# Two query tiles per visit in the dilated attention, fewer statistics stores, and memory gating tied behind row maxima

## The chip, the cores and the metric

The kernel runs on one core of one Trainium2 chip. The core has five engines with instruction streams of their own: TensorE (PE in the profile) for matrix products and transposes, VectorE (DVE), ScalarE (ACT), GpSimd (POOL) and SyncE (SP), which here only issues transfers. They wait for one another through semaphores. PE writes its results to PSUM, which has eight banks of 128 x 512 float32 values; tiles in SBUF are 128 partitions high. The metric is device time in microseconds (us) for one execution, the median over several. A profile is one execution of its own, with its own time.

## The reference, cut to what matters

One encoder block over 1024 tokens of width 1024: a dilated window attention (branch a), a grouped-query attention (b) and an attention into 256 memory slots (m), each gated and projected, merged by gates, and projected once more.

```python
h = rms_norm(x, g_pre)
a_qkv, bq, bk, bv, mq, ga, gb, gm, mg = split(h @ w_in)
# a: three groups (window, dilation) = (128,1), (512,4), (2048,16), 8 heads of 64 each
for gi, (window, dil) in enumerate(A_GROUPS):
    o_g, lse_g = dilated_window_attention(aq[gi], ak[gi], av[gi], window, dil)
    # sc = q k / 8 in the band; m = max sc; p = exp(sc - m); l = sum p; o = p v / l; lse = m + log l
wts = softmax(stack(lses), axis=0)                # over the three groups
oa  = einsum('gbsh,gbshd->bshd', wts, stack(outs))
ob  = softmax(qb kb / 8) vb                       # 8 query heads on 2 key heads, with a row maximum
om  = softmax(qm km / sqrt(128)) vm               # 256 memory slots
ya, yb, ym = (oa*silu(ga)) @ w_a, (ob*silu(gb)) @ w_b, (om*silu(gm)) @ w_m
merged = sigmoid(mg0)*ya + sigmoid(mg1)*yb + sigmoid(mg2)*ym
out = x + rms_norm(merged @ w_out, g_post)
```

## The kernel before

Dense products are made in three terms of high and low parts, so one dense product of a 128 x 512 output is 12 matmuls over four k-blocks. The work stands in stages along the span, and PE carries all of them: the projections of the start, then the grouped-query attention (`b_att`, 222 to 467 us from the start of the span), woven with gate products; the large projections of q, k and v of the dilated branch with the merge gates (467 to 1068 us); the dilated attention, woven with the branch projections `y` (1068 to 1291 us); the remaining `y` products, and the output projection to the end.

A stage with attention is woven from two sources: a generator that yields, between its steps, a cost in TensorE time, and a queue of dense units, whose matmuls fill that cost. In the dilated stage a dense unit (`add_y`) has 24 matmuls in two halves, each half in one bank (`psd`). After a half, `y_evac` is put on a list (`pend`), which is emptied one entry at a time along the stage; it is a multiplication by the gate in place in PSUM, and then an addition to the accumulator, on DVE.

**The dilated stage.** There are twelve items: four pairs of heads times three dilations, named (p_, g). An item has eight query tiles T of 128 rows. For two tiles and two heads, `scores(b)` writes two PSUM banks (`pss1`). `soft(T)` runs on DVE: for each head one custom instruction adds the mask, copies the scores to `pra` and takes the extreme of the row; ACT then takes the exponential with the row sum. `trans(T)` transposes the exponentials on PE into a bank (`pst`) and copies them on DVE to `app`. `pv(b)` multiplies four tiles with the values into one bank (`pst`), which ACT copies to `og`. PSUM holds four banks for scores (`s1=4`), two of `pst` and two of the dense products. `plan(it, pre, nxt)` sets the order: for each T of 0 to 7 a `soft`, then at even T the `scores` of the next two tiles, then `trans` of the tile three back (LAG), then `combining(T)` and `tokens(T)`; `pv` stands at T = 3 and T = 7, `stats` of the item before at T = 2. Each `soft` carries the whole dense filling of its T.

**Statistics and weighing.** `stats` transposes row extremes and sums, and stores them from `sr` to DRAM (`std`) in 4 transfers (g = 0, 2) or 8 (g = 1), from SP, or for g = 2 and for item (3, 1) from ACT. For the pairs 0 to 2 `combine` fetches them back as `cpt`, computes shares, stores them to `wgd`, loads them spread over the partitions (`wgt`, two buffers) and weighs and sums the three outputs on POOL (`weigh`, `gate`), one step where `STEP_T` names that T. For the last pair, `rows` is loaded from `std` in four transfers, two at T = 2 and two at T = 6 of the last item; `shares_3` transposes it and carries on from there while the last `y` products run. `wide`, `first_two` and what follows them apply the weights with banks of `pss1` and `pst`.

**The grouped-query attention.** Per step, PE transposes keys by queries into a bank `tr`, and DVE takes a row maximum from it (`TENSOR_REDUCE bn<-tr`); with the bank still unread the next such product waits. `memory_load(k)` loads the two halves of an output and of a gate of the memory branch, and `memory_gate(k)` multiplies them (tiles `tb` and `tx`) on DVE and stores them. At the step numbers n = 112, 116, 130 and 132 a load is issued, at 128, 129, 137 and 139 a gate of both halves.

The order of the instructions on an engine is fixed when the program is built. `issue_after(x)` holds an instruction behind x in that order.

## Time and profile before

| | |
|---|---|
| median of 3 runs | 1426.65 us (1425.48 to 1427.89) |
| the profiled execution's own time | 1428.24 us |
| its span | 1426.4 us |
| PE busy | 1389.7 us, 97% |
| DVE busy | 1022.1 us, 72% |
| ACT busy | 658.7 us, 46% |
| POOL busy | 573.1 us, 40% |
| transfers | 212.30 MB, mean 149 GB/s |

Busy time of PE counts matmuls whose clock is low as well as those at full clock. The views by time stretch give busy time of each engine with the granted clock; the views of waits say for which instruction an engine stood, with the line that it waited for; the timeline gives single instructions or runs of the same.

### The profile page before, as it was taken

Reading aid. Unit: us, or ns where it says so; the run is one execution under the profiler, and the core shown is the slowest. Engines: PE = TensorE matmul, PEld = TensorE weight load, DVE = VectorE, ACT = ScalarE, POOL = GpSimd, SP = SyncE. Lnnn points to the kernel's source line nnn. Section 1 sums busy time; section 2 is a strip of 40 time slices with the busy share of each in tenths; the row PEclk is TensorE's granted clock in tenths of the full one; section 3 lists DMA queues with packets and bytes.
Section 4 is the critical chain, followed back from the end, with each engine's and each line's share of the span. In section 5 each row is a group of like instructions: output and inputs, shape, how many; then the busy total and the mean of one; then the engine's idle time right before and its main releaser. Section 6 shows DMA issues by size and latency. Waiting matters only on the chain.

```text
span 1426.4 us, 21831 instructions
## 1 busy us (share of the span) xinstructions
PE 1389.7 (97%) x7775; PEld 1110.5 (78%) x7775; DVE 1022.1 (72%) x1828; ACT 658.7 (46%) x1384; POOL 573.1 (40%) x440
## 2 busy tenths in 40 slices
PE   7999999999999999999999999999999999989997
PEld 7799986656656889888888888888887777767886
DVE  7768677767784697676877766677786556657977
ACT  6544365665545444333333333333345665642332
POOL 0416703766656000254565544455541263360003
PEclk9999999999999999999999999999999999999999
DMA  6356532322251787333333233333365577655455
GB/s 234 98 177 213 187 115 74 112 82 79 96 184 49 239 263 235 118 118 119 111 109 96 95 114 104 111 104 119 109 215 191 187 214 206 204 163 179 149 204 177
DMA packets 122013, 212.30 MB, mean 149 GB/s; under 512 B 32592, under 2 KB 61104, under 8 KB 121904
## 3 DMA queue, kind: packets, MB, share of 16 engines
q1 hardware_dynamic: 112240, 196.92, 42.4%
q10 hardware_dynamic: 9664, 14.00, 2.7%
q8 instruction: 61, 1.00, 0.3%
q14 instruction: 48, 0.39, 0.1%
HBM read 144.48 MB, written 66.38 MB: 148 GB/s over the span
## 4 chain that ended last, share of the span: by engine, by line
PE 87%; DVE 5%; ACT 2%; POOL 2%; DMA 2%; issue 2%; ACTq 0%; SPq 0%; DVEq 0%; POOLq 0%
PE s L1322 34%; PE d L1883 5%; PE s L1232 4%; PE s L2107 4%; PE ov L815 4%; PE sc L2025 3%; PE s L1283 3%; PE d L143 3%; PE d L145 3%; PE d L147 3%; PE s L1582 2%; PE tr L1654 2%; PE s L799 2%; PE s L800 2%; PE tr L781 2%
## 5 line engine op out<-in xcount | busy, mean ns | idle before, releaser
L806 POOL TENSOR_TENSOR bl<-bl,bp 128x512 f32<-128x512 f32 x96 | 131.0, 1365 | 59.1 <-ACT bp L802 53.8
L1322 PE MATMUL s<-hh,vS 128*128 128x512 f32 x400 | 133.4, 395 | 0.0
L1322 PE MATMUL s<-vA,vS 128*128 128x512 f32 x450 | 106.6, 390 | 0.0
L106 DVE TENSOR_TENSOR vS<-vot,vS 128x512 fp32r<-128x512 f32 x75 | 86.1, 1149 | 19.9 <-ACT vS L105 19.9
L1322 PEld LDWEIGHTS s<-vA,vS 128*128 128x128 f32 x450 | 84.5, 188 | 18.3
L802 ACT ACTIVATE bp<-s 128x512 f32<-128x512 f32 x128 | 75.9, 596 | 48.7 <-PE s L800 47.6
L1595 ACT ACTIVATE pra<-pra,sts 128x192 f32<-128x192 f32 (+2 forms) x176 | 75.3, 429 | 47.9 <-DVE sts L1594 45.1
L782 DVE TENSOR_REDUCE bn<-tr 128x1 f32<-128x512 f32 x128 | 85.1, 683 | 12.0 <-PE tr L781 10.8
L143 PE MATMUL d<-hh,wh 128*128 128x512 f32 x224 | 90.4, 404 | 2.5 <-DVE fth L216 2.5
L147 PE MATMUL d<-hh,wl 128*128 128x512 f32 x224 | 90.1, 402 | 0.0
L145 PE MATMUL d<-hl,wh 128*128 128x512 f32 x224 | 89.6, 400 | 0.0
L1322 PEld LDWEIGHTS s<-hh,vS 128*128 128x128 f32 x400 | 75.3, 188 | 17.7
L1322 PE MATMUL s<-hl,vS 128*128 128x512 f32 x200 | 79.1, 395 | 0.0
L1322 PE MATMUL s<-hh,wh 128*128 128x512 f32 x200 | 78.4, 392 | 0.0
L1322 PE MATMUL s<-hh,wl 128*128 128x512 f32 x200 | 78.4, 392 | 0.0
L1322 PE MATMUL s<-hl,wh 128*128 128x512 f32 x200 | 77.8, 389 | 0.0
L1633 DVE COPY app<-tr 128x384 f32<-128x384 f32 (+1 forms) x64 | 38.8, 606 | 45.9 <-PE tr L1621 25.2
L1326 ACT ACTIVATE vv<-s 128x512 f32<-128x512 f32 x50 | 30.0, 599 | 85.7 <-PE s L1322 59.2
L1066 POOL TENSOR_TENSOR vot<-wr 128x512 f32<-128x512 f32 x13 | 22.2, 1707 | 111.3 <-DVE wl L106 111.3
L815 PE MATMUL ov<-bp,VS 128*64 128x512 f32 x256 | 58.5, 598 | 0.0
L781 PE MATMUL tr<-KS,QH 128*128 128x512 f32 x128 | 52.2, 407 | 4.7 <-DVE bn L782 3.8
L1356 POOL TENSOR_TENSOR wh<-wr,wh 128x512 fp32r<-128x512 f32 x17 | 21.9, 1289 | 85.6 <-ACT wh L1355 85.6
(627 smaller groups left out, 4078.9 us busy)
## 6 DMA issues: line engine op xcount, KB each, us to landing
wr<-in_wu SPq DMA_DIRECT2D x40, 512.0 KB
vA<-in_wu SPq DMA_DIRECT2D x24, 512.0 KB
qkd<-ko SPq DMA_DIRECT2D x96, 128.0 KB
wl<-thd SPq DMA_DIRECT2D x24, 512.0 KB
wos<-os SPq DMA_DIRECT2D x12, 512.0 KB
wr<-in_wbr SPq DMA_DIRECT2D x24, 256.0 KB
aq<-qkd SPq DMA_DIRECT2D x12, 512.0 KB
ak<-qkd SPq DMA_DIRECT2D x12, 512.0 KB
```

The source lines that it names most:

```text
L106: V.tensor_tensor(dst_l, src, dst_h.bitcast(F32), op=OP.subtract)
L143: PE.matmul(dst, wh[:, k, :], hh[k][:, t], start=k == 0, stop=False)
L145: PE.matmul(dst, wh[:, k, :], hl[k][:, t], start=False, stop=False)
L147: PE.matmul(dst, wl[:, k, :], hh[k][:, t], start=False, stop=k == 7)
L781: PE.matmul(s, QH[:, kv * 4 + j], KS[:, kv, c * 512:c * 512 + 512], start=True, stop=True)
L782: fp["last"] = V.tensor_reduce(st[i]["n"][:, j, c:c + 1], s, axis=AX.X, op=OP.min)
L802: A.activation(pp, s, AF.Exp, scale=-1.0)
L806: G.tensor_tensor(lsum[i % 2], lsum[i % 2], pp, op=OP.add)
L815: PE.matmul(o[e * 64:e * 64 + 64], VS[:, kt, kv], d.pop(kt), start=kt < 2, stop=kt >= NT - 2)
L1322: PE.matmul(BANK[n, c], a, b, start=k == 0 and q == 0 and not more, stop=k == 3 and q == 2, skip_group_check=c in "XW")
L1595: A.activation(src, src, AF.Exp, scale=-1.0, bias=bias, accum_out=sts[:, h, 1, T:T + 1])
L1883: PE.matmul(ps_, a, b, start=k == 0 and q == 0, stop=k == 3 and q == 2)
```

## The change

In the dilated stage `plan` no longer has eight visits of one tile, but four `visit(b)` of two tiles. One visit holds, in this order on PE, `pv` of the item before (at b = 0 and 2), `scores(b)`, and the transposes of two tiles of two visits back; on DVE the four `soft` heads, and then the two copies, which `trans` now returns as a function. `stats` stands at b = 1. Behind a visit two `rest(T)` hold `combining` and `tokens`. A visit has the filling cost of one T of before, each `rest` half of it, so that an item's sum is the same. PSUM is divided anew: two banks for scores instead of four, four of `pst` instead of two. `wide(g, x)` with x = 1 takes a `pst` bank.

Statistics are stored in 4, 4 and 1 transfers for g = 0, 1 and 2, all from SP, to `std` in another order of its dimensions; `rows` is loaded in two transfers of 32 partitions. `weigh` of g = 1 and 2 is split in a multiplication and an addition, each a step of its own, and `STEP_T` has 14 entries. The evacuation of a `y` half with an accumulation is two entries of the list `pend` instead of one. In `b_att`, each half of a memory gate is a call of its own, at n = 115 to 134, and is held behind the row maximum that was last issued.

```diff
-            std = dram.tile([4, 2, 3, 2, S], F32, name="std")
+            std = dram.tile([4, 3, 2, 2, S], F32, name="std")
...
-        def memory_gate(k):
-            for j, (o, g) in enumerate(zip(*MT.pop(k))):
+        def memory_gate(k, j):
+            o, g = [x[j] for x in MT[k]]
+            with tc.issue_after(fp["last"].ins):
                 V.scalar_tensor_tensor(o, o, 0.5, g, op0=OP.mult, op1=OP.mult)
-                nc.sync.dma_start(od[2, k, :, half[j]], o)
+            nc.sync.dma_start(od[2, k, :, half[j]], o)
+        MEMORY = {108: (0,), 110: (1,), 115: (0, 0), 117: (0, 1), 119: (1, 0), 121: (1, 1), 122: (2,), 124: (3,),
+                  129: (2, 0), 130: (2, 1), 133: (3, 0), 134: (3, 1)}
...
-    phase_psum("ps_a", s1=4, t=2)
-    pss1()
+    phase_psum("ps_a", s1=2, t=4)
...
-                V.tensor_copy(pp[:, :k], tp[:, :k])
                 st[T] = terms
+                return lambda: V.tensor_copy(pp[:, :k], tp[:, :k])
...
-                E = nc.scalar if g == 2 or (p_, g) == (3, 1) else nc.sync
+                dst = std[p_, g].rearrange("s h x -> (s h) x")
+                if g == 0:
+                    for z in range(4):
+                        nc.sync.dma_start(dst[z].rearrange("(b t a) -> t b a", b=16, t=8),
+                                          sr[8 * z:8 * z + 8].rearrange("p (b a) -> p b a", b=16))
+                elif g == 1:
+                    for z in range(4):
+                        nc.sync.dma_start(dst[z].rearrange("(e t a) -> t e a", e=4, t=8),
+                                          sr[8 * z:8 * z + 8].rearrange("p (e a) -> p e a", e=4))
+                else:
+                    nc.sync.dma_start(dst.rearrange("z (t a) -> (z t) a", t=8), sr)
...
+            def visit(b):
+                if pre and b in (0, 2):
+                    pre["pv"](b // 2)
+                if it:
+                    it["scores"](b)
+                at = it if b > 1 else pre
+                copies = [at["trans"](2 * ((b + 2) % 4) + j) for j in range(2)] if at and (it or b < 2) else []
+                if it:
+                    it["soft"](2 * b)
+                    it["soft"](2 * b + 1)
+                for f in copies:
+                    f()
+                if b == 1 and pre and it:
+                    pre["stats"]()
+                if not it:
+                    shares_3(b)
+                    return
+                if b in (0, 2):
+                    it["values"](b // 2)
+                if b == 2 and pre:
+                    ready()
+                if b == 3 and it["ahead"]:
+                    qk_fetch(*it["ahead"])
+            def rest(T):
+                combining(T)
+                tokens(T)
+            for b in range(4):
+                out.append((lambda b=b: visit(b), SOFT + 100.0 if it else LAST_PAD))
+                if it:
+                    out += [(lambda T=T: rest(T), 0.5 * SOFT + 50.0) for T in (2 * b, 2 * b + 1)]
...
-        STEP_T = (4, 0, 1, 1, 2, 6, 6, 7, 2, 3, 4, 6)
+        STEP_T = (4, 0, 1, 1, 2, 5, 6, 7, 7, 0, 3, 4, 5, 7)
...
-                    pend.append(lambda t=t, ps_=ps_: y_evac(m, t, ps_))
+                    pend.extend([lambda t=t, ps_=ps_, z=z: y_evac(m, t, ps_, (z,)) for z in range(1 if n == 0 else 2)])
...
-            W3B[g, x] = pst().rearrange("p a b -> p (a b)") if g == 2 else pss1()
+            W3B[g, x] = pst().rearrange("p a b -> p (a b)") if g == 2 or x else pss1()
```

The order of instructions shows three places. The first is PE in an item with g = 0 or 1, around a `pv`; `s` is a score product, `tr<-cs,pra` a transpose, `tr<-app,avs` and `avp` the outputs, `d` the dense products. Before:

```order
L1621 MATMUL tr<-cs,pra 128x128 x3
L1883 MATMUL d<-hh_86,wh 128x512
L1883 MATMUL d<-hh_87,wh 128x512
L1883 MATMUL d<-hl_95,wh 128x512
L1621 MATMUL tr<-cs,pra 128x128 x3
L1654 MATMUL tr<-app,avs 64x128 x14
L1654 MATMUL tr<-app,avp 64x128 x2
L1883 MATMUL d<-hh_87,wh 128x512
L1883 MATMUL d<-hh_88,wh 128x512
L1883 MATMUL d<-hl_96,wh 128x512
L1582 MATMUL s_10739<-ak,aq 128x128
L1582 MATMUL s_10740<-ak,aq 128x192
```

And the same item after:

```order
L1880 MATMUL d<-hh_88,wh 128x512
L1880 MATMUL d<-hl_96,wh 128x512
L1659 MATMUL tr<-app,avs 64x128 x14
L1659 MATMUL tr<-app,avp 64x128 x2
L1587 MATMUL s_10707<-ak,aq 128x128
L1587 MATMUL s_10708<-ak,aq 128x192
L1587 MATMUL s_10707<-ak,aq 128x64
L1587 MATMUL s_10707<-ak,aq 128x192
L1587 MATMUL s_10708<-ak,aq 128x128
L1587 MATMUL s_10708<-ak,aq 128x64
L1626 MATMUL tr<-cs,pra 128x128 x6
L1880 MATMUL d<-hh_88,wh 128x512
```

Outputs, scores and the transposes of two tiles now follow one another, with the dense products before and behind them. The second place is DVE in `b_att` near the first memory gates (`tx`, `tb`); `bn<-tr` are the row maxima, `QL` a part of the query preparation. Before:

```order
L106 TENSOR_TENSOR bll<-bl_2695,blh 128x512
L767 SCALAR_TENSOR_TENSOR tb_4576<-tb_4576,tb_4578 128x512
L717 TENSOR_TENSOR QL<-tr,QH 64x4x128 x2
L767 SCALAR_TENSOR_TENSOR tx_4520<-tx_4520,tx_4521 128x512 x2
L818 TENSOR_TENSOR obt<-obt,ov 64x512
L767 SCALAR_TENSOR_TENSOR tb_4577<-tb_4577,tb_4579 128x512
L782 TENSOR_REDUCE bn_4380<-tr 128x1 x2
```

After:

```order
L786 TENSOR_REDUCE bn_4529<-tr 128x1
L768 SCALAR_TENSOR_TENSOR tx_4446<-tx_4446,tx_4447 128x512
L786 TENSOR_REDUCE bn_4529<-tr 128x1 x2
L768 SCALAR_TENSOR_TENSOR tx_4446<-tx_4446,tx_4447 128x512
L106 TENSOR_TENSOR bll<-bl_2694,blh 128x512
L216 SCALAR_TENSOR_TENSOR fth<-d,fth 128x512
L822 TENSOR_TENSOR obt<-obt,ov 64x512
L786 TENSOR_REDUCE bn_4529<-tr 128x1 x2
L768 SCALAR_TENSOR_TENSOR tb_4492<-tb_4492,tb_4494 128x512
```

The gates stand singly with row maxima between them. The third place is SP near the end of the last item; `rows<-std` is the load that `shares_3` needs, `wgt<-g2d` loads a gate, `wl<-thd` and `wr` serve the `y` products. Before:

```order
L1524 DMA avs<-vdr 64x8x64 x2
L1825 DMA wgt<-g2d 128x1024
L1726 DMA rows<-std 16x128 x2
L1524 DMA avs<-vdr 64x8x64 x2
L1350 DMA wr<-in_wbr 128x512
L1363 DMA wl<-thd 128x1024
L1723 DMA wgt<-g2d 128x1024
L1726 DMA rows<-std 16x128 x2
```

After:

```order
L1529 DMA avs<-vdr 64x8x64 x2
L1822 DMA wgt<-g2d 128x1024
L1687 DMA std<-sr 8x4x32 x4
L1723 DMA rows<-std 32x128
L1352 DMA wr<-in_wbr 128x512
L1529 DMA avs<-vdr 64x8x64 x2
L1365 DMA wl<-thd 128x1024
L1720 DMA wgt<-g2d 128x1024
L1723 DMA rows<-std 32x128
```

The four stores now stand on SP ahead of the first load of `rows`, and the second load keeps its place behind the same large transfers.

More of the change, by code (lines that the diff above doesn't have):

```diff
@@ L858, in b_att @@
                     yield 109
-                if n in (112, 116, 130, 132):
-                    memory_load((112, 116, 130, 132).index(n))
-                if n in (128, 129, 137, 139):
-                    memory_gate((128, 129, 137, 139).index(n))
+                if n in MEMORY:
+                    (memory_gate if len(MEMORY[n]) > 1 else memory_load)(*MEMORY[n])
                 m = n - LAG_T
@@ L1363, in th_load, with y_evac @@
             nc.sync.dma_start(THS[m], thd[8 * i + f])
-    def y_evac(m, t, ps_):
+    def y_evac(m, t, ps_, parts=(0, 1)):
         n, i, f = steps[m]
@@ L1368, in y_evac @@
         if n == 0:
+            if 0 not in parts:
+                return
             if accs[f] is None:
@@ L1372, in y_evac @@
         else:
-            V.scalar_tensor_tensor(ps_, th[:, t], 1.0, ps_, op0=OP.add, op1=OP.mult)
-            V.tensor_tensor(accs[f][:, t], ps_, accs[f][:, t], op=OP.add)
+            if 0 in parts:
+                V.scalar_tensor_tensor(ps_, th[:, t], 1.0, ps_, op0=OP.add, op1=OP.mult)
+            if 1 in parts:
+                V.tensor_tensor(accs[f][:, t], ps_, accs[f][:, t], op=OP.add)
     def qk_first(x):
@@ L1591, in soft @@
                     src = pr[:, h * n:h * n + n]
-                    bias = sts[:, h, 0, T:T + 1]
+                    bias = sts[:, 0, h, T:T + 1]
                     m0 = 384 + 192 * h if turned(T, h) else mo
                     fp["last"] = V.tensor_tensor_reduce(src, sv[h], mask[:, m0:m0 + n], 1.0, 3.0e38, OP.add, OP.min, bias)
-                    A.activation(src, src, AF.Exp, scale=-1.0, bias=bias, accum_out=sts[:, h, 1, T:T + 1])
+                    A.activation(src, src, AF.Exp, scale=-1.0, bias=bias, accum_out=sts[:, 1, h, T:T + 1])
                 st[T] = pr
@@ L1607, in trans @@
                             st[T - 1 + z] = pp[:, z]
-                        V.tensor_copy(pp[:, :2], tp[:, :2])
-                    return
+                        return lambda: V.tensor_copy(pp[:, :2], tp[:, :2])
+                    return lambda: None
                 pr = st[T]
@@ L1674, in stats @@
                     A.activation(sr, tp[0:32, 0, :], AF.Copy)
-                E = nc.scalar if g == 2 or (p_, g) == (3, 1) else nc.sync
-                for h in range(2):
-                    for q in range(2):
-                        row = sr[(h * 2 + q) * 8:(h * 2 + q) * 8 + 8]
-                        dst = std[p_, h, g, q]
-                        if g == 0:
-                            E.dma_start(dst.rearrange("(b t a) -> t b a", b=16, t=8),
-                                              row.rearrange("p (b a) -> p b a", b=16))
-                        elif g == 1:
-                            for f in range(2):
-                                E.dma_start(dst.rearrange("(e r f a) -> f r e a", e=4, r=4, f=2)[f],
-                                                  row[f:f + 7:2].rearrange("p (e a) -> p e a", e=4))
-                        else:
-                            E.dma_start(dst.rearrange("(t a) -> t a", t=8), row)
+                dst = std[p_, g].rearrange("s h x -> (s h) x")
[9 more added lines that the diff above has]
+                    nc.sync.dma_start(dst.rearrange("z (t a) -> (z t) a", t=8), sr)
             return dict(
@@ L1692, in item @@
                 ahead=seq[p_ * 3 + g + 2] if p_ * 3 + g + 2 < len(seq) else None,
-                values=[(lambda x=x: values(x), 0.0) for x in range(2)],
-                scores=[(lambda b=b: scores(b), 0.0) for b in range(4)],
-                soft=[(lambda T=T: soft(T), SOFT + 100.0) for T in range(NT)],
-                trans=[(lambda T=T: trans(T), 0.0) for T in range(NT)],
-                pv=[(lambda b=b: pv(b), 0.0) for b in range(2)],
-                stats=(stats, 0.0))
+                values=values, scores=scores, soft=soft, trans=trans, pv=pv, stats=stats)
         def plan(it, pre, nxt):
@@ L1724, in tokens @@
                     if T in (2, 6):
-                        for j in (0, 1) if T == 2 else (2, 3):
-                            nc.sync.dma_start(rows[16 * j:16 * j + 16],
-                                              std[3, j % 2, j // 2].rearrange("s (t a) -> (s t) a", t=NT))
+                        j = T // 6
+                        nc.sync.dma_start(rows[32 * j:32 * j + 32], std[3, j].rearrange("s h (t a) -> (s h t) a", t=NT))
             def ready():
@@ L1731, in ready @@
                     todo.extend(combine(pre["key"][0], [OG.pop((pre["key"][0], x)) for x in range(3)]))
-            if it and not pre:
-                out += it["scores"][:2]
-            for T in range(NT if it else 4):
+            def visit(b):
+                if pre and b in (0, 2):
+                    pre["pv"](b // 2)
                 if it:
-                    out.append(it["soft"][T])
-                if T == 2 and pre and it:
-                    out.append(pre["stats"])
-                if T % 2 == 0 and (it or T == 0):
-                    x = {0: pre and it and it["scores"][1], 2: it and it["scores"][2], 4: it and it["scores"][3],
-                         6: nxt and nxt["scores"][0]}[T]
-                    if x:
-                        out.append(x)
-                if T < LAG:
-                    if pre:
-                        out.append(pre["trans"][T + 8 - LAG])
-                elif it:
-                    out.append(it["trans"][T - LAG])
-                out.append((lambda T=T: combining(T), 0.0))
-                out.append((lambda T=T: tokens(T), 0.0) if it else (lambda T=T: shares_3(T), LAST_PAD))
-                if T == 3:
-                    if pre:
-                        out.append(pre["pv"][1])
-                    if it:
-                        out.append(it["values"][1])
-                    if pre and it:
-                        out.append((ready, 0.0))
-                if T == 5 and it and it["ahead"]:
-                    out.append((lambda: qk_fetch(*it["ahead"]), 0.0))
-                if T == 7:
-                    out.append(it["pv"][0])
-                    if nxt:
-                        out.append(nxt["values"][0])
@@ new lines, in visit @@
+                    it["scores"](b)
[10 more added lines that the diff above has]
+                    shares_3(b)
+                    return
@@ L1787, in fetch @@
                 for h in range(2):
-                    E.dma_start(c["t"][h * 64:h * 64 + 64], std[p_, h].rearrange("g s (i e) -> i g s e", e=16))
+                    E.dma_start(c["t"][h * 64:h * 64 + 64].rearrange("p g s e -> p (g s) e"), std[p_, :, :, h].rearrange("g s (i e) -> i (g s) e", e=16))
             def shares():
@@ L1811, in put, with weigh @@
                     E.dma_start(wgd[p_, h].rearrange("g (i e) -> i g e", e=16), c["e"][h * 64:h * 64 + 64])
-            def weigh(g):
+            def weigh(g, add=False):
                 wv = wgt[g].rearrange("p (b a) -> p a b", b=16)
                 ogv, og0 = [z.rearrange("p (a b) -> p a b", b=16) for z in (ogs[g], ogs[0])]
-                G.tensor_tensor(ogv, ogv, wv, op=OP.mult)
-                if g:
+                if add:
                     G.tensor_tensor(og0, og0, ogv, op=OP.add)
+                else:
+                    G.tensor_tensor(ogv, ogv, wv, op=OP.mult)
             def gate():
@@ L1833, in combine @@
             return [fetch, shares, weights, put, lambda: [load(0), load(1)], lambda: weigh(0), lambda: weigh(1),
-                    lambda: load(2), load_gate, lambda: weigh(2), gate, store]
+                    lambda: weigh(1, True), lambda: load(2), load_gate, lambda: weigh(2), lambda: weigh(2, True), gate, store]
         todo = []
-        STEP_T = (4, 0, 1, 1, 2, 6, 6, 7, 2, 3, 4, 6)
+        STEP_T = (4, 0, 1, 1, 2, 5, 6, 7, 7, 0, 3, 4, 5, 7)
         seq = [(p_, g) for p_ in range(4) for g in range(3)]
@@ L1891, in first @@
         def first():
-            items[0]["values"][0][0]()
             yield FIRST_PAD
@@ L1923, in shares_3 @@
                 V.tensor_copy(c3[:, 0:2].rearrange("p g h s t -> p (g h s t)"), C["b"][:, 0:64])
-                V.tensor_tensor(mn, b[:, 0:4].rearrange("p (g h) (s t) -> p g h s t", g=2, s=2)[:, 0, :, 0], c3[:, 1, :, 0], op=OP.min)
-                V.tensor_tensor(mn, mn, c3[:, 2, :, 0], op=OP.min)
-                V.tensor_tensor(eg, c3[:, :, :, 0], mn[:, None].to_broadcast([P, 3, 2, NT]), op=OP.subtract)
+                V.tensor_tensor(mn, b[:, 0].rearrange("p (h t) -> p h t", h=2), c3[:, 1, 0], op=OP.min)
+                V.tensor_tensor(mn, mn, c3[:, 2, 0], op=OP.min)
+                V.tensor_tensor(eg, c3[:, :, 0], mn[:, None].to_broadcast([P, 3, 2, NT]), op=OP.subtract)
                 A.activation(eg, eg, AF.Exp, scale=-1.0)
@@ L1930, in shares_3 @@
                 b = C["b"][:, 0:192].rearrange("p (x y) -> p x y", x=12)
-                V.tensor_tensor(b[:, 8:11].rearrange("p g (h t) -> p g h t", h=2), eg, c3[:, :, :, 1], op=OP.mult)
+                V.tensor_tensor(b[:, 8:11].rearrange("p g (h t) -> p g h t", h=2), eg, c3[:, :, 1], op=OP.mult)
                 ds_ = cb.tile([P, 16], F32, name="cds", bufs=2)
```

## The prediction

> **What bounds the kernel now.** I read the page first, then the table of time stretches, then what PE waits for in the stages that the change touches, and last the timelines around those waits. The page gives the busy shares:

> ```profile
> span 1426.4 us, 21831 instructions
> PE 1389.7 (97%) x7775; PEld 1110.5 (78%) x7775; DVE 1022.1 (72%) x1828; ACT 658.7 (46%) x1384; POOL 573.1 (40%) x440
> ```

> PE is the bound. A change that removes no matmul can therefore win only where PE stands, where it steps slowly, or where its clock is low. The stretches (columns: length, busy time of PE, PEld, DVE, ACT, POOL with instruction counts, granted clock, DMA share, GB/s) show where that is:

> ```profile
> 222.00:467.00 245.00, 240.16 (x1031) 153.40 (x1030) 173.53 (x264) 140.58 (x233) 151.58 (x112) 0.99 0.28 95
> 467.00:1068.00 601.00, 601.00 (x2778) 499.00 (x2777) 446.08 (x521) 231.22 (x368) 248.65 (x149) 1.00 0.44 141
> 1068.00:1297.00 229.00, 215.85 (x2023) 164.53 (x2021) 141.97 (x569) 128.20 (x461) 85.44 (x42) 0.98 0.63 193
> 412.10:418.90 6.80, 5.13 (x13) 3.91 (x14) 4.81 (x9) 1.69 (x3) 2.26 (x3) 0.50 0.49 130
> 1272.30:1279.10 6.80, 4.29 (x12) 3.32 (x13) 3.40 (x12) 0.94 (x4) 0.00 (x0) 0.50 0.30 104
> 1296.20:1303.00 6.80, 5.74 (x14) 4.51 (x15) 6.63 (x12) 3.75 (x7) 0.00 (x0) 0.50 0.95 356
> ```

> From 467 to 1068 us PE has no gap, and the change touches nothing there. The grouped-query stage (first row) has 4.8 us without PE work, the dilated stage (third row) 13.2 us. The last three rows are stretches with the clock at half. What PE waits for, in three windows (400 to 467, 1268 to 1305, and 1072 to 1268 us; total, times, longest):

> ```profile
> PE tr L781 <- DVE bn L782: 3.3, 1, 3.3
> ...
> PE s L1922 <- DMA rows<-std: 5.1, 1, 5.1
> PE sc L2025 <- DVE og L1968: 3.1, 1, 3.1
> ...
> PE tr L1621 <- DVE app L1633: 2.2, 3, 1.3
> PE s L1582 <- DVE sts L1594: 1.0, 1, 1.0
> PE tr L1647 <- DVE app L1633: 0.7, 1, 0.7
> PE tr L1606 <- ACT pra L1595: 0.6, 2, 0.3
> PE s L1575 <- DVE sts L1594: 0.5, 1, 0.5
> ```

> Three single waits of 3.3, 5.1 and 3.1 us, and small ones of 5.0 us in all. Each of the three is followed by one of the half-clock stretches. What half clock costs shows in the chain of waits: six dense matmuls behind the second wait took 2.86 us, six shortly after it 1.40.

> ```profile
> 1268.23 6.29 DMA rows<-std
> ...
> 1274.81 0.34 PE s L1922
> 1275.15 2.86 PE d L1883 x6
> ...
> 1280.29 1.40 PE d L1883 x6
> ```

> So a half-clock stretch loses half of the PE busy time in it: 2.6, 2.1 and 2.9 us by the rows above. The three places together cost 3.3 + 2.6 = 5.9, 5.1 + 2.1 = 7.2, and 3.1 + 2.9 = 6.0 us.

> [...]

> **The change, part by part.** *Memory gates.* The first wait is DVE's doing. Its timeline there:

> ```profile
> 407.80 1.39 DVE L717 TENSOR_TENSOR QL<-tr,QH 64x512 fp32r<-64x512 f32 x2 [2.13 <-ACT QH L714]
> 409.22 2.23 DVE L767 SCALAR_TENSOR_TENSOR tx<-tx,tx 128x512 f32<-128x512 f32 x2
> 411.48 0.68 DVE L818 TENSOR_TENSOR obt<-obt,ov 64x512 f32<-64x512 f32 x1
> 412.08 1.03 DVE L767 SCALAR_TENSOR_TENSOR tb<-tb,tb 128x512 f32<-128x512 f32 x1
> 413.04 1.28 DVE L782 TENSOR_REDUCE bn<-tr 128x1 f32<-128x512 f32 x2
> ```

> Three gate halves, 2.23 + 1.03 us, stand between the maxima that PE waits for: just the 3.3 us that it stood. In the new order each half follows one row maximum, so a later maximum is delayed by one half (0.7 to 1.1 us), not by three. Gain: at most 5.9 us; at least none, if a gate halts DVE on its load, which is issued only some seven steps earlier. Near the end three halves still stand ahead of one `QL`. I take 5.5.

> *Fewer changes of kind on PE.* In the order, dense matmuls are resumed behind other work 88 times before and 48 times after, from the first scores to the transpose of `rows`. The price of one, from a stretch of PE's timeline:

> ```profile
> 1195.44 0.39 PE L1654 MATMUL tr<-app,avp 128*64 128x128 f32 x4
> 1195.76 0.50 PE L1883 MATMUL d<-bl,wh 128*128 128x512 f32 x1
> 1196.10 0.63 PE L1883 MATMUL d<-bh,wh 128*128 128x512 f32 x2
> 1196.56 0.40 PE L1883 MATMUL d<-bl,wh 128*128 128x512 f32 x1
> 1196.89 1.04 PE L1582 MATMUL s<-ak,aq 64*128 64x128 f32 x12
> 1197.86 0.55 PE L1621 MATMUL tr<-cs,pra 128*128 128x128 f32 x3
> 1198.16 0.71 PE L1883 MATMUL d<-bh,wh 128*128 128x512 f32 x2
> 1198.71 0.39 PE L1883 MATMUL d<-bl,wh 128*128 128x512 f32 x1
> 1198.94 0.49 PE L1621 MATMUL tr<-cs,pra 128*128 128x128 f32 x3
> ```

> A dense matmul steps by 0.23 us (1198.71 to 1198.94, 1196.10 to 1196.56 for two). The first behind outputs takes 0.34 (1195.76 to 1196.10), two behind transposes 0.55 instead of 0.46, the last ahead of scores 0.33. An interruption thus costs about 0.1 us at one of its ends: 40 x 0.1 = 4.0 us. Outputs directly ahead of scores, 22 times, have no row; by the nearest, 0.33 against 0.23, they cost the same 0.1, which is in those that remain on either side. Ends: 0, and 6 if both ends of an interruption count where outputs are moved.

> *Scores with one pair of banks.* `scores(b+1)` now waits for both `soft` of the same pair of banks, in the visit just before, no longer for those of two visits before. The rows for DVE:

> ```profile
> L1594 DVE CUSTOM_DVE_ANT_0 pra<-s,mask x192: 211/349/422, 1073.8 to 1266.3; 128x192 f32<-128x192 f32 x80, 128x64 f32<-128x64 f32 x64, 128x256 f32<-128x256 f32 x48
> L1633 DVE COPY app<-tr x64: 550/558/692, 1079.4 to 1259.0; 128x384 f32<-128x384 f32 x40, 128x512 f32<-128x512 f32 x24
> ```

> DVE needs 4 x 0.35 = 1.4 us for the softs of a visit. PE meanwhile has two tiles' transposes (six or eight, some 0.6 us by 0.30 per three) and six to eight dense matmuls (8 x 0.23 = 1.8): 2.0 to 2.4 us, and 1.8 more where `pv` comes first. So 0.6 to 1.0 us is left at half of the visits. A copy (0.56) or one evacuation ahead of the softs fits; both do not. I put 2.5 us for new waits here; ends 0, and 36 visits x 0.5 = 18.

> *Small waits.* The five rows above (5.0 us) stand where copies or softs are late. Copies now come a visit ahead of `pv`, behind which four `pst` banks instead of two wait: I take 2 us of the 5 as gone (ends 0 and 5).

> *Stores, loads of `rows`, and weighing.* Eight stores of item (3, 1) held up ACT, and SP waited for them before its next loads:

> ```profile
> 1259.08 5.32 ACTq L1685 DMA_DIRECT2D std<-sr  x8
> 1264.44 0.35 ACT L1595 ACTIVATE pra<-pra,c 128x64 f32<-128x64 f32 x1 [5.39 <-DVE c L1594]
> ...
> SPq L1524 <- DMA std<-sr: 2.4, 1, 2.4
> ...
> L1685 SPq DMA_DIRECT2D std<-sr x24: 589/590/754, 1110.1 to 1215.2; - x24
> ```

> Now ACT issues none, and four stand on SP: 4 x 0.59 = 2.4 us there, as much as the wait of SP that goes, but at an earlier step. What is won is ACT's 5.3 us: exponentials stood behind the stores, the outputs behind those, and the load of the next values, two places ahead of `rows` on SP, behind the outputs. I expect the second `rows` load about 4 us earlier (between 0 and 5.3). The two halves of a `weigh` leave the order of the transfers ahead of it as it is. PE has about 0.6 us less work between that load's place and the transpose of `rows`, since two tiles' transposes and the outputs are through earlier. So 5.1 - 4 + 0.6 = 1.7 us remain; behind a wait of 1.3 us, the longest of the small ones, no half-clock stretch stands, and I count none here. Gain 7.2 - 1.7 = 5.5 us, which I take. Ends: 0, if the load goes out as late as before, and 7.2.

> *The evacuation in two entries.* The same two instructions, but the bank is released later, some three steps of dense work before its next use. It costs nothing as long as DVE is not behind; if it is, the price is up to one 0.7 us operation for each of eight units, 5.6 us. I take 0.5.

> *The third wait.* The product at L2025 waits for a combine chain on DVE whose instructions are the same. DVE is busy for 6.63 of the 6.80 us in the third half-clock row. Nothing here makes it shorter: 0.

> **Sum:** 5.5 + 4.0 + 2.0 + 5.5 - 2.5 - 0.5 = 14.0 us. The profiled execution took 1428.2 us, so 1414.2 by its own time. It stood 1.6 us above the median of 1426.65, which gives 1412.6 for the median.

> **Rivals.** (A) *Slower: single score banks.* DVE's queue falls behind in most visits, and each `scores` waits. For it: 0.6 us of slack at half the visits, and 142 us of DVE work in 229. Against it: single waits of PE for softs were two in the whole stage, 1.5 us. It decides against the change from about 0.4 us per visit over 36 visits beyond what I took (14.0 us); at 0.55 us (19.8) the time is 1432.4.

> (B) *The `rows` wait stays.* SP now issues the stores itself, the second load stays behind wr, wl and wgt, and the 6.29 us from issue to landing is mostly the queue of large transfers. PE, arriving earlier, stands as long: 5.5 us of the sum go, 1418.1. A middle case, with 2 to 3 us left and the low clock with it, ends near 1415.

> (C) *The gates halt DVE on their loads.* The wait moves from three gates in a row to single ones: 5.5 us go, 1418.1.

> (D) *Changes of kind are not worth their price* and the new waits eat the rest: only gates and `rows` pay (11.0 us), 1415.6.

> (E) *The planning does not take effect*: B, C and D at once, 1426 to 1428.

> **How the numbers follow.** My forecast, 1405 to 1415.5: 0.50. B 0.14, C 0.09, D 0.10, all faster. A 0.13, of which 0.10 lies above 1429.5 and 0.03 within the band; E 0.04, half within the band and half faster. A measurement of this kernel tells 0.2% (2.9 us) from no change. So faster 0.85, same 0.05, slower 0.10. The range takes in B, C and D and a part of A: 1402 (all gains at their upper ends but the third wait: 5.9 + 6 + 5 + 7.2 = 24.1) to 1424.

> **What would show it.** Right: in the grouped-query stage PE is without the 3.3 us wait and the 0.50 clock near 412 us; the dilated stage shrinks from 229 us by 9 to 10; the wait for `rows` is at most 1.5 us, and the clock stays full behind it; the wait at L2025's successor is still about 3 us. Wrong: rows that say PE `s` waits for DVE `sts` many times (A); the `rows` wait at 3 to 5 us (B); DVE waits for transfers at the gates (C); a dilated stage with few waits, but no shorter (D).

## The result and the profile after

The changed kernel takes 1413.94 us in the median of four runs (1412.71 to 1415.53), the kernel before 1426.78 us. The ratio is 0.9911, with a 95% interval of 0.9894 to 0.9928: 12.8 us faster. The forecast was 1412.6, in a range of 1402 to 1424. The profiled execution is one of 1412.7 us, against 1428.2 before. The page of the changed kernel begins:

```profile
span 1410.9 us, 21845 instructions
...
PE 1379.7 (98%) x7775; PEld 1106.2 (78%) x7775; DVE 1025.7 (73%) x1828; ACT 658.5 (47%) x1384; POOL 574.7 (41%) x440
```

PE still bounds the kernel. What it waits for between 150 and 1340 us (total, times, longest):

```profile
PE sc L2021 <- DVE og L1964: 2.7, 1, 2.7
PE d L1880 <- DMA wgt<-wgd: 2.2, 1, 2.2
PE tr L1659 <- DVE app L1639: 1.7, 1, 1.7
PE s L1918 <- issue: 1.0, 1, 1.0
PE d L1880 <- DVE acc L1380: 0.9, 1, 0.9
PE s L804 <- DVE QL L794: 0.9, 1, 0.9
...
PE tr L785 <- DVE bn L786: 0.7, 2, 0.5
PE tr L793 <- DVE bnm L788: 0.4, 1, 0.4
```

The waits of 3.3 us for row maxima and 5.1 us for `rows` are gone (what is left of the latter is the 1.0 us at L1918), and the third, now 2.7, is there. But three new ones stand in the dilated stage (2.2, 1.7, 0.9) and one in the grouped-query stage (0.9). Four lines mark the stages; each row has the first and the last start of a group. Before, the first large projection, the first `y` product, the transpose of `rows` and the first product of the tail:

```profile
L1232 PE MATMUL s<-wh,hh x56: 389/389/393, 467.6 to 538.5; 128*128 128x512 f32 x56
L1883 PE MATMUL d<-hh,wh x128: 387/396/504, 1067.7 to 1176.1; 128*128 128x512 f32 x128
L1922 PE MATMUL s<-cs,rows x1: 338/338/338, 1274.8 to 1274.8; 64*128 64x64 f32 x1
L2025 PE MATMUL sc<-hh,wh x96: 387/389/467, 1291.2 to 1340.9; 128*128 128x512 f32 x96
```

And after:

```profile
L1234 PE MATMUL s<-wh,hh x56: 389/389/393, 464.7 to 535.7; 128*128 128x512 f32 x56
L1880 PE MATMUL d<-hh,wh x128: 387/395/496, 1064.8 to 1168.0; 128*128 128x512 f32 x128
L1918 PE MATMUL s<-cs,rows x1: 243/243/243, 1264.2 to 1264.2; 64*128 64x64 f32 x1
L2021 PE MATMUL sc<-hh,wh x96: 387/389/467, 1278.9 to 1325.4; 128*128 128x512 f32 x96
```

Up to the projections 2.9 us are won; from there to the `y` products nothing (600.1 us in both); from the first `y` product to the transpose of `rows` 7.8 (207.1 to 199.3); from there to the tail 1.7 (16.4 to 14.7); in the tail's own products, first to last start, 3.2 (49.7 to 46.5). The last two, 4.9 us, are mostly low clocks that did not come in this execution; in three of the kernels below, with the same stores and the same tail, they came (a half-clock stretch that starts between 1265.7 and 1267.5 us, and in two of them another at 1288; the granted clock of the three was 0.993 to 0.995, that of the changed kernel 0.996). That makes 15.5 us by this pair of executions, while the medians differ by 12.8.

To part the 207.1 and 199.3 us, PE's steps (the time from the start of one matmul to the start of the next) were sorted by the kinds of the two matmuls; what a step has over the largest usual one of its kind counts as a wait, and half of a step at half clock as lost to the clock. That gives (in us):

| kernel | steps without waits | waits in the stage | half clock | wait for `rows` |
|---|---|---|---|---|
| before | 195.0 | 6.6 | 0 | 5.5 |
| changed | 190.9 | 5.6 | 1.5 | 1.3 |

So the steps fell by about 4.0 us and the wait for `rows` by 4.2, while the waits are other ones than before but hardly less. Where a step ends and a wait begins is a choice. If only the idle times that the profile lists as waits are taken off (5.0 us in both kernels), and 1.7 us for the half clock, 196.6 us are left before and 191.3 after: 5.3 us less.

### The profile page after: what moved, and what is told of

Read it like the earlier page. It is cut to its first block, busy times and chain, and to the rows that moved or that the text cites. A ratio compares the mean times of both kernels' runs of the same rounds, so it can differ in the third digit from the quotient of the medians.

```text
span 1410.9 us, 21845 instructions
## 1 busy us (share of the span) xinstructions
PE 1379.7 (98%) x7775; PEld 1106.2 (78%) x7775; DVE 1025.7 (73%) x1828; ACT 658.5 (47%) x1384; POOL 574.7 (41%) x440
## 4 chain that ended last, share of the span: by engine, by line
PE 87%; DVE 4%; POOL 3%; ACT 2%; issue 2%; DMA 1%; SPq 0%; DVEq 0%; POOLq 0%; ACTq 0%
PE s L1324 34%; PE d L1880 5%; PE s L1234 4%; PE s L2103 4%; PE ov L819 4%; PE sc L2021 3%; PE s L1285 3%; PE d L145 3%; PE d L147 3%; PE d L143 3%; PE s L1587 2%; PE s L804 2%; PE tr L1659 2%; PE s L803 2%; PE tr L785 2%
## 5 line engine op out<-in xcount | busy, mean ns | idle before, releaser
L1324 PE MATMUL s<-hh,vS 128*128 128x512 f32 x400 | 133.4, 395 | 0.0
L1324 PE MATMUL s<-vA,vS 128*128 128x512 f32 x450 | 106.6, 390 | 0.0
L1599 DVE CUSTOM_DVE_ANT_0 pra<-s,mask 128x192 f32<-128x192 f32 (+2 forms) x192 | 52.7, 326 | 69.3 <-PE s L1587 34.7
L1324 PEld LDWEIGHTS s<-vA,vS 128*128 128x128 f32 x450 | 84.5, 188 | 18.3
L1324 PEld LDWEIGHTS s<-hh,vS 128*128 128x128 f32 x400 | 75.3, 188 | 17.7
L1324 PE MATMUL s<-hl,vS 128*128 128x512 f32 x200 | 79.1, 395 | 0.0
L1324 PE MATMUL s<-hh,wh 128*128 128x512 f32 x200 | 78.4, 392 | 0.0
L1324 PE MATMUL s<-hh,wl 128*128 128x512 f32 x200 | 78.4, 392 | 0.0
L1324 PE MATMUL s<-hl,wh 128*128 128x512 f32 x200 | 77.8, 389 | 0.0
L1068 POOL TENSOR_TENSOR vot<-vot,vA 128x512 f32<-128x512 f32 x12 | 19.3, 1608 | 90.8 <-DVE vS L106 90.8
L143 PEld LDWEIGHTS d<-hh,wh 128*128 128x128 f32 x224 | 42.2, 188 | 14.9 <-issue 5.5
```

What stands on the lines that cost most here:

```text
L143: PE.matmul(dst, wh[:, k, :], hh[k][:, t], start=k == 0, stop=False)
L1324: PE.matmul(BANK[n, c], a, b, start=k == 0 and q == 0 and not more, stop=k == 3 and q == 2, skip_group_check=c in "XW")
```

## The experiments

**Gates alone.** The kernel before with the new gates and no other edit (`memory_gate(k, j)` tied behind the last row maximum, and the table `MEMORY`, as in the diff of the change).

> The kernel before with the new memory gates alone. Theory from the two traces: the wait of 3.3 us near 410 us and the half clock behind it go (5 us), and about 2 us come back where gates stand ahead of the last QL, so the first large projection starts at about 464.7 us instead of 467.6, and the time is some 2.9 us shorter, 1423.8. Rival, the term of the prediction (5.5 us): the projection starts at 462.1 and the time is 1421.3. In both, the wait for rows (5.1 us) and the wait at the combine chain (3.1 us) stay as before.

It took 1422.31 us, ratio 0.9968 (0.9956 to 0.9979): 4.4 us faster than before. The median lies nearer to the rival's 1421.3 than to 1423.8, and the first projection starts at 463.7 us, between the two marks. But both contain what the edit does not touch: in this execution the start of the kernel was 1.2 us shorter, and the half clock in the tail came for one stretch of 3.4 us instead of 6.8. From the first product for a row maximum to the first projection, which leaves these out, before takes 247.8 us, this 245.1, the changed kernel 245.0: 2.7 us, near the theory's 2.9. Against before, PE is 5.05 us ahead one group of outputs behind the old wait, and then loses 0.6 and 1.7 us in the two groups that follow. Where the 1.7 go, the changed kernel's timelines of DVE, GpSimd and PE show:

```profile
440.73 1.24 DVE L788 TENSOR_TENSOR bnm<-bn 128x4 f32<-128x4 f32 x1
441.89 0.68 DVE L768 SCALAR_TENSOR_TENSOR tx<-tx,tx 128x512 f32<-128x512 f32 x1
442.50 1.79 DVE L768 SCALAR_TENSOR_TENSOR tb<-tb,tb 128x512 f32<-128x512 f32 x1
444.31 0.69 DVE L794 TENSOR_TENSOR QL<-tr,cs 4x512 fp32r<-4x512 f32 x1
...
440.59 6.50 POOL L810 TENSOR_TENSOR bl<-bl,bp 128x512 f32<-128x512 f32 x4 [0.34 <-ACT bp L806]
...
445.06 0.50 PE L804 MATMUL s<-QL,KB 68*128 68x512 f32 x1 [0.85 <-DVE QL L794]
```

Two gate halves (0.68 and 1.79 us) stand directly ahead of the `QL` for which PE waits. They stand beside GpSimd's additions `bl`, which is the likely cause of their length: one of the two equal halves takes 1.79 us, and the small `bnm`, which ends at 441.97, 0.03 us behind an addition, 1.24 us, where the median of its 16 executions is 0.16.

**Last gates later.** The changed kernel, with

```diff
-                V.tensor_tensor(QQ[T][1][64:68, ...
+                fp["ql"] = V.tensor_tensor(QQ[T][1][64:68, ...
...
-            with tc.issue_after(fp["last"].ins):
+            with tc.issue_after(fp["ql" if k > 1 else "last"].ins):
...
-                  129: (2, 0), 130: (2, 1), 133: (3, 0), 134: (3, 1)}
+                  131: (2, 0), 133: (2, 1), 135: (3, 0), 137: (3, 1)}
```

> The changed kernel with the last four gate halves held behind the last QL instead of the last row maximum. Theory: the 0.9 us wait for QL and the 0.4 us wait for bnm go with what follows them, and the first large projection starts at 463.0 to 463.5 us instead of 464.65. Rival: those waits come from GpSimd's additions that hold up VectorE, not from the order; then the start stays within 0.3 us of 464.65.

Both waits went, and the same stretch took 244.0 us instead of 245.0: the 1.7 us were won back, and 0.7 of them lost again behind, 0.4 at the next outputs. The first projection started at 464.2, later than the 463.0 to 463.5 expected, also because this execution's start of the kernel was 0.6 us longer. The order put the halves ahead of `QL`; their length there goes, by the rows above, with GpSimd's additions. The whole kernel took 1417.9 us in its one execution, more than the changed kernel, since 2 us of other waits and three low clocks, not one, fell into the dilated stage and the tail.

**GpSimd's subtraction later.** In the dilated stage the 1.7 us wait is that of an output product for a copy, and the copy stands behind one small operation on VectorE. The changed kernel's VectorE, GpSimd and TensorE there:

```profile
1234.39 2.38 DVE L1803 SCALAR_TENSOR_TENSOR ceg<-ceg,cds 128x48 f32<-128x48 f32 x1
...
1234.33 2.38 POOL L1861 TENSOR_TENSOR hl<-hl,hh 128x1024 fp32r<-128x1024 f32 x1 [8.77 <-DMA avp<-vdr]
...
1238.54 0.90 PE L1659 MATMUL tr<-app,avs 128*64 128x128 f32 x12 [1.68 <-DVE app L1639]
```

The same line takes 0.21 us in its other two executions. The edit:

```diff
-                if n in (9, 10) and T < 3:
-                    dl_high(n - 9, half[T]) if T < 2 else dl_low(n - 9)
+                if n in (9, 10) and 3 <= T < 6:
+                    dl_high(n - 9, half[T - 3]) if T < 5 else dl_low(n - 9)
```

> The changed kernel with the GpSimd subtraction hl<-hl,hh of the items 9 and 10, and the copies it needs, three steps later. Theory: the small ceg operation on VectorE took 2.38 us because that subtraction ran at the same time; moved, ceg takes 0.21 us everywhere, the wait of the outputs for copies (1.7 us) goes, and the dilated stage (first y product to the first product of the tail) takes about 212.2 us instead of 214.05. Rival: VectorE is behind by its own work in that visit; then a wait of 1 us or more stays at that place although ceg is short.

The wait for the copy is no longer in the list, and line L1803 takes 0.21 us in all three executions, so the cause is shown: the subtraction held VectorE up. But the stage did not reach 212.2 us: up to the last step before `rows` it took 197.4 us (198.0 in the changed kernel), since other waits of 1.1 us came, and up to the tail 216.2, because the wait for `rows` had grown from 1.0 to 2.2 us, with a low clock behind it. The kernel took 1411.7 us in its one execution.

**Stores on ScalarE again.** The changed kernel with one edit:

```diff
+                E = nc.scalar if g == 2 or (p_, g) == (3, 1) else nc.sync
...
-                        nc.sync.dma_start(dst[z]...
+                        E.dma_start(dst[z]...
```

> The changed kernel with the statistics stores of g = 2 and of item (3, 1) issued from ScalarE again (1 and 4 instead of 8, no other edit). Theory: the stores on ScalarE were what made the load of rows late; four of them still cost ScalarE 2.4 us and the wait for rows is back with 1.5 to 3 us. Rival: the load became early by the moved values and outputs, and the wait for rows stays under 0.5 us; then the stage from the first y product to the transpose of rows stays within 0.5 us of 199.3.

The waits of PE in it:

```profile
PE s L1919 <- issue: 3.5, 1, 3.5
PE d L1881 <- POOL wh L1358: 2.8, 2, 1.9
```

The wait for `rows` is 3.5 us instead of 1.0, and the half clock stands behind it for 6.8 us. That is a little over the 1.5 to 3 us of the theory and well off the rival. With eight stores it was 5.1. So the stores on ScalarE do lengthen the wait. How much of the 4.1 us is theirs is less sure than the 2.5 us of this pair: in the other kernels here that store from SP the wait is 0.7 to 2.6 us, and 2.0 and 1.3 in two executions of one of them. The kernel took 1419.2 us in its one execution. The second row has the new 2.2 us wait too (1.9 here), and names GpSimd's `wh` for it, where the changed kernel's list names a transfer of `wgt`.

**Transposes apart.** One tile's transposes go out of the visit into the `rest` behind it, so that dense work is resumed 94 times instead of 48.

```diff
-  copies = [at["trans"](2 * ((b + 2) % 4) + j) for j in range(2)] if at and (it or b < 2) else []
+  copies = [at["trans"](2 * ((b + 2) % 4) + j) for j in range(1 if it else 2)] if at and (it or b < 2) else []
...
             def rest(T):
+                at = it if T > 3 else pre
+                if T % 2 == 0 and at:
+                    at["trans"]((T + 4) % 8 + 1)()
                 combining(T)
```

> The changed kernel with the second tile's transposes and copy moved out of the visit into the first rest behind it. Dense work is now resumed 94 times instead of 48. Theory (an interruption of the dense products costs 0.1 us): PE's steps in the dilated stage without its waits grow by 4.6 us (4 to 5.5). Rival: grouping saves no step time and the stage got shorter by fewer waits; then the steps without waits stay within 1 us and only waits differ.

The steps without waits did not grow by 4.6 us. By the sorting above they fell by 1.4, to 189.5; with only the listed waits taken off they grew by 1.0, to 192.3. By either count the theory falls, and the rival too, since the steps did fall from before to after. The kernel took 1408.3 us in its one execution, without a low clock from the first `y` product to the tail. PE's timeline of the kernel before, two rows further than the prediction quotes it, says why:

```profile
1199.19 0.71 PE L1883 MATMUL d<-bh,wh 128*128 128x512 f32 x2
1199.73 0.40 PE L1883 MATMUL d<-bl,wh 128*128 128x512 f32 x1
```

Three transposes between dense matmuls take 0.25 us to the next dense start (1198.94 to 1199.19), and the two dense matmuls behind them 0.54 instead of 0.46: 0.33 in all, three steps of the 0.11 us that transposes have among themselves. Behind scores the three take 0.30 and the dense ones 0.55, 0.06 us more. In these rows transposes interrupt dense work for nothing, or nearly so. What costs is a dense matmul behind outputs: 0.34 us instead of 0.23. That happened 22 times before, with 0.34 us on average, and never after: 22 x 0.11 = 2.4 us of the 4.0 to 5.3. Outputs ahead of scores, which took their place, cost nothing: in the changed kernel the scores behind outputs take 0.39 us (1195.76 to 1196.15), as those behind dense matmuls do (1198.59 to 1198.98). The last dense matmul ahead of scores or outputs also takes 0.33 us, but that happened 44 times before and 49 after, so it wins nothing. The rest was not parted further.

**The evacuation in one entry.** The changed kernel with

```diff
-  pend.extend([lambda t=t, ps_=ps_, z=z: y_evac(m, t, ps_, (z,)) for z in range(1 if n == 0 else 2)])
+  pend.append(lambda t=t, ps_=ps_: y_evac(m, t, ps_))
```

> The changed kernel with the evacuation of a y half in one entry again. Theory: the wait of a dense product for acc (0.9 us) comes from the addition that now stands behind softs and copies; in one entry it goes, nothing else moves, and the stage from the first y product to the transpose of rows without the wait for rows falls from 198.3 to about 197.4 us. Rival: two operations in a row (1.4 us on VectorE) hold up softs, and waits of PE for sts or app of 1 us or more appear in its place.

This was the surprise: 1404.4 us in the one execution, 8 us less than the changed kernel's profiled execution. The steps to the transpose of `rows` took 192.8 us, not 197.4, and all three new waits of the dilated stage were gone or short. Timed again:

> The kernel with the evacuation in one entry again, timed. Theory: the two-entry list fills the slots in which the splits of the next weights were issued, so that GpSimd makes wh behind the weighing; undone, the changed kernel gains 6 to 10 us, a median of 1404 to 1408. Rival: the single look at 1404.4 owed most of its gain to low clocks that happened to stay away; then the median is 1409 to 1412.

1405.42 us (1402.34 to 1410.40), ratio to before 0.9855 (0.9833 to 0.9877). Undoing this one part gains 8.5 us. By the profiled executions (1410.9 and 1403.6 us of span) 4.8 of 7.3 us lie in the dilated stage ahead of the wait for `rows`, and 2.3 in the tail, where the third wait is 0.4 us instead of 2.7; what shortened that one is open. For the dilated stage, the changed kernel's GpSimd and TensorE show the reason at the 2.2 us wait:

```profile
1193.70 5.85 POOL L1815 TENSOR_TENSOR og<-og,wgt 128x1024 f32<-128x1024 f32 x2 [15.49 <-DMA wgt<-wgd]
1199.62 2.38 POOL L1813 TENSOR_TENSOR og<-og 128x1024 f32<-128x1024 f32 x1
1201.96 1.26 POOL L1358 TENSOR_TENSOR wh<-wr,wh 128x512 fp32r<-128x512 f32 x1
...
1200.72 0.40 PE L1880 MATMUL d<-bl,wh 128*128 128x512 f32 x1
1203.28 0.51 PE L1880 MATMUL d<-bh,wh 128*128 128x512 f32 x1 [2.15 <-DMA wgt<-wgd]
```

The weight part `wh` ends at 1203.22, and PE goes on at 1203.28. It stood behind three weighing operations, 8.2 us. With the evacuation in one entry, GpSimd has it behind the first:

```profile
1192.85 2.91 POOL L1815 TENSOR_TENSOR og<-og,wgt 128x1024 f32<-128x1024 f32 x1 [15.78 <-DMA wgt<-wgd]
1195.73 1.28 POOL L1358 TENSOR_TENSOR wh<-wr,wh 128x512 fp32r<-128x512 f32 x1
1196.98 2.93 POOL L1815 TENSOR_TENSOR og<-og,wgt 128x1024 f32<-128x1024 f32 x1
1199.99 2.37 POOL L1813 TENSOR_TENSOR og<-og 128x1024 f32<-128x1024 f32 x1
```

The list `pend` is emptied one entry at a time, and it holds not the evacuations alone, but also the loads and the split of the next weights. Two entries more per unit, one for each half, move all of these.

**The split ahead in the list.** To part the two effects, the evacuation stays in two entries and the split goes to the head:

```diff
-                    pend.append(lambda: y_split(m + 1, G))
+                    pend.insert(0, lambda: y_split(m + 1, G))
```

> The changed kernel, evacuation still in two entries, but the split of the next weights put at the head of the list. Theory: wh is then ahead of the weighing on GpSimd, the 2.2 us wait of a dense product and the low clock behind it go, and the stage from the first y product to the transpose of rows, without that last wait, takes about 194.5 us instead of 198.05; the wait for acc (1.0 us) stays or grows to 2. Rival: the wait came from the late release of the dense bank; then 2 us or more of waits for DVE acc or d stand in its place.

The 2.2 us wait went, with its low clock, but the stage took 197.8 us. In its place stand

```profile
PE d L1880 <- DVE acc L1380: 3.2, 3, 1.5
```

which is what the rival named: now the dense bank is released late. So the list is short of slots, as far as these two runs tell: whichever entry goes ahead, the other is late. A list that is emptied faster was not tried. The kernel took 1412.9 us in its one execution.

**Weighing later.** The changed kernel with `STEP_T = (4, 0, 1, 1, 2, 6, 7, 0, 0, 1, 3, 4, 5, 7)`, the weighing of g = 0 and 1 a step or two later.

> The changed kernel with the weighing of g = 0 and 1 one to two steps later (6, 7, 0, then the load at 0 and the gate's load at 1). Theory: the 2.2 us wait of a dense product is for the weight part wh that GpSimd makes behind three weighing operations in a row; with the steps later it stands ahead of them, the wait falls under 0.5 us, the low clock behind it goes, and the stage without the wait for rows takes 195.5 to 196.5 us instead of 198.3. Rival: the gate's load is now late and holds up the loads behind it on SP, so that the wait for rows is 2 us longer than 1.0.

This run took 7775 us, with PE slower throughout, also in the stages that the edit doesn't touch: a 128x512 matmul of L1324 is listed with 1.69 us, in the changed kernel with 0.39, at a granted clock of 1.00. The trace does not say why, and the same kernel was run again.

> The kernel with the late weighing steps again, since in its first run every engine's work for PE stood still for a reason outside the kernel (PE stepped five times slower in stages that no edit touches). Theory as before: the 2.2 us wait falls under 0.5 us, and the stage without the wait for rows takes 195.5 to 196.5 us instead of 198.05. Rival: the wait for rows gets 2 us longer.

1419.2 us in its one execution. The wait for `wh` did not go: it stands at two other places with 1.8 and 1.0 us, and the stage took 198.5 us. The wait for `rows` was 1.6 us. Neither the theory nor the rival held; here moving GpSimd's operations among themselves only moved the place at which PE waited for them.

**PSUM as before.** The changed kernel with `s1=4, t=2` and `wide(g, 1)` in a score bank.

> The changed kernel with PSUM divided as before (four banks for scores, two for transposes and outputs). Theory: single score banks cost nothing (no wait for sts in the profile after), while with two banks the second tile's transposes wait for the copy of the outputs by ScalarE, 0.3 to 0.6 us at 22 visits, so the stage grows by 6 to 13 us. Rival (A of the prediction): the single score banks cost, and the stage gets shorter by 1 us or more.

1427.0 us in its one execution: the gain is gone. The wait that makes it:

```profile
PE tr L1673 <- DVE app L1640: 14.8, 8, 4.5
```

The size, 14.0 us more in the stage, is a little over the 6 to 13 of the theory, and the place is another: what waits is the transpose of the statistics, at eight visits, for the copies of that visit, not the second tile for the outputs (ScalarE's `og`, 1.4 us). So the visits need the new division of PSUM. That single score banks cost nothing rests on the list after the change, which has no wait for `sts`; with the score banks doubled again, the steps without the listed waits are no shorter either (192.2 us to 191.3).

**Both at once.** The evacuation in one entry, and the last gates later:

> The evacuation in one entry and the last four gate halves held behind the last QL, together. Theory: the two edits touch different stages and add up, 1.0 us less than the evacuation alone, 1403 to 1407 in the median. Rival: loads shift with the gates (the single look with the late gates had 0.7 us of new waits in the dilated stage), and the median is not below that of the evacuation alone.

1403.99 us (1402.24 to 1404.57), ratio to before 0.9841 (0.9827 to 0.9854). That is 10.0 us under the changed kernel and the shortest median here. Against the evacuation alone it is 1.4 us less in the median, and 1.0 us less in the stretch from the first product for a row maximum to the first projection (244.1), but the intervals of the two overlap. Its longest waits between 150 and 1340 us:

```profile
PE s L1918 <- issue: 1.6, 1, 1.6
PE tr L1652 <- DMA avs<-vdr: 1.1, 1, 1.1
PE d L1880 <- POOL wh L1358: 0.7, 1, 0.7
...
PE sc L2021 <- DVE og L1964: 0.4, 1, 0.4
```

The third wait, which was to stay, is 0.4 us here as in the kernel with the evacuation alone, and absent with the subtraction later or the transposes apart. With the subtraction later, the product with `ak` starts at 1283.34 us, ahead of the VectorE read (from 1285.39) that held it in the changed kernel, and the next one, with `aq`, at 1286.22, 0.15 us behind that read, with no change in the order of the instructions there. That points to another PSUM bank for the product; it was not tested by itself.

## Why the prediction was right, point by point

- **The whole.** 14.0 us were forecast, 12.8 measured. By the pair of executions it is 2.7 (gates) + 4.0 (steps) + 1.0 (waits in the dilated stage, 6.6 to 5.6) - 1.5 (half clock there) + 5.9 (`rows`: 4.2 for the wait, 1.7 behind it) + 3.2 (tail) = 15.3 us, and 0.2 at the start of the kernel. The tail was forecast at nothing and the gates at twice what they gave; these two misses offset each other, so that the total came so close is partly luck. The terms for gates, `rows` and fewer changes are there with their signs, and the new waits took what the small ones gave.
- **Memory gates, 5.5.** The wait and its low clock went as said: 5.05 us, for 5.9 counted. But the halves ahead of `QL` cost 2.3 us (0.6 and 1.7) and not the 0.4 that I had put on them, the 1.7 beside GpSimd's additions, so that 2.7 remained. They were named as the place; the term was mis-sized, by 2.8 us.
- **Fewer changes of kind, 4.0.** Measured 4.0 or 5.3, as one counts, but by another mechanism; that the number fits is luck. The step that failed is "an interruption thus costs about 0.1 us": 46 more interruptions cost between -1.4 and 1.0 us, not 4.6. A price shows on dense work behind outputs, for 2.4 us; the rest is open. The price that the prediction gave to outputs ahead of scores does not show either.
- **Single score banks, -2.5.** No wait for `sts` is in the list after. The term was 0, and rival A did not come about.
- **Small waits, 2.0.** The old ones went (6.6 us by the sorting), more than forecast, and 5.6 us of new ones came. Together with the terms for score banks and evacuation, -1.0 us was forecast for waits, and +1.0 came, or -0.5 with the half clock.
- **Stores and `rows`, 5.5.** The wait fell from 5.1 to 1.0 us, and its low clock went: 5.9 us. The mechanism, stores off ScalarE, is borne out by the run that put them back. That the clock stayed is less firm: three of the other kernels that store from SP had 3.4 us of half clock behind waits of 1.5 to 2.2 us here.
- **The evacuation in two entries, -0.5.** Here the working failed, and the range did not show it because other terms made up for it. "It costs nothing as long as DVE is not behind" looked at the bank alone. The list's other entries, the split of the next weights above all, come later too, and undoing it gains 8.5 us in the medians. Even the upper end of 5.6 us was too low.
- **The third wait, 0.** Still there with 2.7 us in the changed kernel, as said. That it can go when another stage is ordered differently I had not seen.
- **Low clocks.** One of 3.4 us was left in the profile after, behind the new 2.2 us wait; the one in the tail, which I had left as it was, did not come there.

## What to carry to other kernels

A list that is emptied at a fixed rate is a resource: splitting one entry delays the ones behind it, whatever it is that they issue, and the cost can show on engines that the edit does not name. Price an interruption on TensorE from the first step before it to the first ordinary step behind it; one step alone shows only where the cost is booked. And when an edit gathers many parts, undo each once: here one of them held back two fifths of what the whole could give.

## What the runs showed of the hardware

```profile
1281.80:1284.50 2.70, 0.00 (x1) 0.01 (x1) 2.63 (x6) 0.00 (x0) 0.00 (x0) 1.00 0.99 305
...
1288.28 0.76 PE L2021 MATMUL sc<-hh,ak 128*128 128x512 f32 x1 [2.76 <-DVE og L1964]
...
1288.00:1291.40 3.40, 3.12 (x8) 2.48 (x8) 3.23 (x6) 1.78 (x4) 0.00 (x0) 0.50 1.02 384
```

Where the edges fall is also a likely cause of the 2 to 3 us between executions of one kernel; the separate executions have no trace here, so that was only argued, but the granted clock of each is on record and fits: of 20 executions of the kernel before, the five slowest (1428.2 to 1428.9 us) had 0.990 to 0.991, the five fastest (1424.0 to 1425.7) 0.991 to 0.995.

**VectorE and GpSimd held each other up.** A VectorE operation of 0.21 us took 2.38 us, and ended 0.06 us behind the GpSimd operation of 2.38 us that had begun 0.06 us before it; in the run in which the subtraction was moved, it took 0.21 us. The delay is that of the other operation, not of the small one. It went both ways: beside the memory gates of the grouped-query stage, where VectorE's halves take up to 1.79 us, GpSimd's four additions take 6.50 us together, where the median of all 96 is 1.29 us, 5.2 for four.
